# A bidirectional encoder layer on one core: the short convolution's matrices kept, the modulation's tail moved, rows of y loaded one step ahead

## The chip, the cores and the metric

One NeuronCore of a Trainium2 chip runs the whole kernel. The metric is device time in microseconds, the median of several executions. The engines are TensorE (PE, with its weight loads PEld), VectorE (DVE), ScalarE (ACT), GpSimd (POOL) and SyncE (SP), whose queue issues nearly all DMAs here, one after the other.

## The reference, cut to what matters

One layer runs over two sequences, the long one (A, 1024 rows) and the short one (B, 512 rows), with the same weights and width 1024. For each of them:

```
mod = silu(c) @ ada_w + ada_b          # six sections of 1024: sh1 sc1 gt1 sh2 sc2 gt2
u   = rmsnorm(x) * (1 + sc1) + sh1
z   = u @ w_in                         # hyena part, q, k, v, two gates
y_hy = x0 * long_conv(x1 * v, filter)  # FFT convolution over the whole length
y_at = dilated_attention(q, k, v)
h   = x + gt1 * ((g_hy * (y_hy @ w_hy_br) + g_at * (y_at @ w_at_br)) @ w_out)
out = h + gt2 * (relu(u2 @ w_up)**2 @ w_down),   u2 = rmsnorm(h) * (1 + sc2) + sh2
```

## The kernel before, in words

**Products.** Every product is a list of *units*, one unit for 128 output columns. A unit's weights (512 KB) are loaded by SP, split by ACT (L401, a rounded high part) and DVE (L402, the rest), and multiplied in three passes (`mm3`, L768: high by high, high by low, low by high). `stream` walks over the units in the order qkvA and zhyA mixed, gateA, qkvB, zhyB, gateB, mixA, mixB, ffA, ffB. At the start of unit i it splits the weights of unit i+1, then issues unit i's matmuls.

**Side work.** Filters, convolutions, attention, norms, the modulation's rest and loads are generators (`Side`). Between the matmuls of a unit `pump` advances a model clock and lets the first side in the list that is ready issue its next step; `yield c, lat` says what the step costs TensorE and how long the side then isn't ready. `finish` drives a side to its end, moving the model clock on where nothing is ready. A side started with `first=True` stands ahead of the others. This walk sets the program order. ACT executes exactly in program order; for the other engines and for SP a scheduler orders the instructions by that priority and its own estimate of what is ready, and each engine then executes its list strictly in order.

**Buffers.** Most working tiles are one kind, `g`, with 36 buffers of 128x1024 floats; a tile's buffer is given to a later tile when its last reader is done, and that later tile's writer waits for it. The DFT matrices of the convolutions are tiles `cm` with 4 buffers.

**Convolution.** `conv_gen(S, th)` handles a third (256) of the channels; three thirds per sequence, one at a time. `stage1` transposes and does a small DFT; `middle(eg)` loads the intermediate (L921), the filter's spectrum (L971, L972), a forward and a backward matrix (`cmat`, L907 to L910, 256 KB each), multiplies (L984), combines on DVE (L985 to L988), multiplies back (L995), copies on ACT (L388) and writes to DRAM (L1001); then the result is read again (L1008), finished by matmuls L1020 and DVE L1024 and stored as `yhy`. The long sequence has four `eg` per third, the short one two, and every third loads the same matrices again.

**Modulation.** The first two sections are computed at the head. `ada_rest` (L613), started at the first unit of gateA, does the other four: it loads both condition rows, applies silu (ACT L619, DVE L620), then takes 32 steps, each one load of 512 KB (L625) a step ahead and two reductions on DVE (L636, one per sequence). The first unit of mixA's output product waits for its end (`finish(H["ada"])`).

**y.** `load_y(S)` (L1419) brings the convolution's six result tiles back: one DMA (L1425), a pause of 3 us of the model clock, then the split on ACT and DVE. For the long sequence it is started at gateB's unit 12 of 16 and must be through before the first unit of mixA.

Of the kernel before, what the change touches and what calls it, by code (L numbers as in the profile page):

```python
# [337 lines left out]
def _program(ctx, tc, d, outs):  # L338
# [10 lines left out]
    dma = nc.sync.dma_start  # L349
# [14 lines left out]
    def nm(s):  # L364
        cnt[0] += 1
        return f"{phase[0]}__{s}{cnt[0]}"

    def g(shape=(1024,), dt=F32):
        return gp.tile([128, *shape], dt, tag="g", name=nm("g"))
# [7 lines left out]
    def pss2():  # L377
        return pss().rearrange("p (a b) -> p a b", a=2)
# [6 lines left out]
    def copy(out, in_):  # L385
        rr[0] += 1
        if rr[0] % CPM:
            A.copy(out, in_)  # L388
        else:
            V.tensor_copy(out, in_)  # L390
# [4 lines left out]
    def table(name):  # L395
        if held[0] != name:
            A.preload_act_table_set(name)
            held[0] = name

    def split(raw, hi, lo, eng=None):  # L400
        A.copy(hi, raw)  # L401
        (eng or V).tensor_tensor(lo, raw, hi.bitcast(F32), ALU.subtract)  # L402
# [131 lines left out]
    SA, SB = Seq(), Seq()  # L534
# [76 lines left out]
        return mm.ins  # L611

    def ada_rest():  # L613
        csl = [g((1024,)) for _ in range(2)]
        for i in range(2):
            sg = g((1024,))
            dma(csl[i], d["cc"][i:i + 1].broadcast_to([128, 1024]))
            table(SIGMOID)
            A.activation(sg, csl[i], AF.Sigmoid)  # L619
            V.tensor_tensor(csl[i], csl[i], sg, ALU.mult)  # L620
        wt = []

        def load(c):
            t = g((1024,))
            dma(t, d["ada"][c - 16])  # L625
            wt.append(t)

        load(16)
        yield 0.0, 5.0
        for c in range(16, 48):  # L630
            if c < 47:
                load(c + 1)
            junk = g((1024,))
            w = wt.pop(0)
            for i in range(2):
                V.tensor_tensor_reduce(junk, w, csl[i], 1.0, adab[:, c:c + 1], ALU.mult, ALU.add, ada[:, i, c:c + 1])  # L636
            yield 0.0, LADA
        ada_scale(1)

    def ada_scale(n, k0=0, nk=8):  # L640
        gg = (n1g, n2g)[n]
        sc = 8 * (1, 4)[n] + k0
        for i in range(2):
            V.scalar_tensor_tensor(modA[:, n, i, k0:k0 + nk], ada[:, i, sc:sc + nk], 1.0, gg[:, k0:k0 + nk],
                                   ALU.add, ALU.mult)
# [181 lines left out]
    def filt_third(S, th, sall, fwo):  # L827
# [62 lines left out]
        def stage2(eg):  # L890
            sin = stage2_load(S, s1, eg)
            cm = cmat(S.fw, eg)
            yield 0.0, LLD
            so = g((4, 256))
            for ep in range(2):
                ps = pss2()
                for ee in range(2):
                    e = 2 * ep + ee
                    T.matmul(ps[:, ee], cm[:, e], sin[:, e], start=True, stop=True)
                V.tensor_tensor(so[:, 2 * ep:2 * ep + 2], ps, rn.unsqueeze(1).broadcast_to([128, 2, 256]), ALU.mult)  # L900
                yield 0.9, 0.0
            dma(S.spec[th][:, 4 * eg:4 * eg + 4], so)

        yield from par([stage2(eg) for eg in range(nt // 4)], WS2)
        yield 0.0, 3.0

    def cmat(src, eg):  # L907
        cm = wp.tile([128, 4, 128], F32, tag="cm", name=nm("cm"), bufs=4)
        dma(cm, src[eg])
        return cm  # L910

    def stage2_load(S, s1, eg):

        Q, nt = S.Q, S.nt
        nl = 64 // Q
        v = s1.rearrange("j p c -> (j p) c").rearrange("(q r l e) c -> r l q e c", q=Q, r=2, l=nl, e=nt)
        t = g((4, 256))
        for r in range(2):
            for l in range(nl):
                p0 = 64 * r + Q * l  # L920
                dma(t[p0:p0 + Q], v[r, l][:, 4 * eg:4 * eg + 4])  # L921
        return t
# [4 lines left out]
    def conv_gen(S, th):  # L927
# [38 lines left out]
        def middle(eg):  # L966
            sin = stage2_load(S, s1, eg)
            ka, kb = g((4, 256)), g((4, 256))
            es = slice(4 * eg, 4 * eg + 4)
            for hf in range(2):  # L970
                dma(ka[64 * hf:64 * hf + 64], S.spec[th][0:64, es])  # L971
                dma(kb[64 * hf:64 * hf + 64], S.spec[th][64:128, es])  # L972
            if eg == 0:
                V.tensor_copy(ka[64:65, 0], kb[0:1, 0])
                V.memset(kb[0:1, 0], 0.0)
                V.memset(kb[64:65, 0], 0.0)
            cm, cb_ = cmat(S.fw, eg), cmat(S.bw, eg)
            yield 0.0, LLD
            y, vv = g((4, 256)), g((4, 256))
            for ep in range(2):  # L980
                e2 = slice(2 * ep, 2 * ep + 2)
                ps = pss2()
                for ee in range(2):
                    T.matmul(ps[:, ee], cm[:, 2 * ep + ee], sin[:, 2 * ep + ee], start=True, stop=True)  # L984
                V.tensor_tensor(y[:, e2], ps, ka[:, e2], ALU.mult)  # L985
                V.scalar_tensor_tensor(vv[0:64, e2], ps[64:128], -1.0, kb[0:64, e2], ALU.mult, ALU.mult)
                V.tensor_tensor(vv[64:128, e2], ps[0:64], kb[64:128, e2], ALU.mult)
                V.tensor_tensor(y[:, e2], y[:, e2], vv[:, e2], ALU.add)  # L988
                yield 0.9, LY if ep else 0.0
            del sin, ka, kb, vv  # L990
            so = g((4, 256))
            for ep in range(2):
                ps = pss2()
                for ee in range(2):
                    T.matmul(ps[:, ee], cb_[:, 2 * ep + ee], y[:, 2 * ep + ee], start=True, stop=True)  # L995
                copy(so[:, 2 * ep:2 * ep + 2], ps)
                yield 0.9, 0.0
            for r in range(2):
                for l in range(nl):
                    p0 = 64 * r + Q * l  # L1000
                    dma(v2[r, l][:, 4 * eg:4 * eg + 4], so[p0:p0 + Q])  # L1001

        yield from par([middle(eg) for eg in range(nt // 4)], WMID)
        bt = []
        v3 = s2.rearrange("(j q) r c -> (q r) j c", q=4)
        for jg in range(J // 4):
            t = g((4, 256))
# [410 lines left out]

    def load_y(S):  # L1419
        S.yh, S.yl = Feat(S, F32R), Feat(S, F32R)  # L1420
        for k in range(6):
            if k == 5 and S is SA:
                S.gl = {0: load_gate(S, 0)}
            t = g((S.L,))
            dma(t, S.yhy[k])  # L1425
            yield 0.0, 3.0
            split(t, S.yh(k), S.yl(k))

    def load_gate(S, m):
        gs = []  # L1430
        for b in range(2):
            t = g((S.L,))
            dma(t, S.gt[2 * m + b])
            gs.append(t)
        return gs
# [136 lines left out]
    H = {}  # L1572
# [25 lines left out]
    def g0():  # L1598
        H["ada"] = start("ada", ada_rest())
# [28 lines left out]
    def yA():  # L1628
        finish(*(H["convA", th] for th in range(3)), H["combA"])
        H["yA"] = start("mixA", load_y(SA), True)  # L1630
# [11 lines left out]
    def o6():  # L1642
        finish(*(H["convB", th] for th in range(3)), H["combB"])
        H["yB"] = start("mixB", load_y(SB), True)
# [85 lines left out]
def build(arrays):  # L1730
    nc = bacc.Bacc("TRN2", target_bir_lowering=False, num_devices=1)
    d = {n: nc.dram_tensor(n, a.shape, mybir.dt.from_np(a.dtype), kind="ExternalInput").ap()
         for n, a in arrays.items()}
    outs = [nc.dram_tensor(n, s, F32, kind="ExternalOutput").ap()
            for n, s in (("out_a", (8, 128, LA)), ("out_b", (8, 128, LB)))]
    with tile.TileContext(nc) as tc:
        with ExitStack() as ctx:
            ctx.enter_context(tc.manual_schedule(engines={mybir.EngineType.Activation}))
            _program(ctx, tc, d, outs)
    return nc  # L1740
# [10 lines left out]
```

## Time and profile before

| what | value |
|---|---|
| three executions | 2626.16, 2627.82 (median), 2630.31 us |
| profiled execution, its own time | 2630.32 us |
| its span | 2628.5 us, so 1.8 us lie around it |
| mean granted TensorE clock over the span | 0.99 |
| TensorE busy | 2562.4 us (97%) |
| VectorE / ScalarE / GpSimd busy | 1248.1 / 860.8 / 152.0 us |
| moved by DMA | 351.06 MB, mean 134 GB/s |

TensorE is busy almost all the time, so little is left to shares; what can change is read from the few stretches in which it stands still, and from the stretches behind them in which its granted clock is 0.50, that is 1.2 instead of 2.4 GHz. The product stages lie at 647 to 861 us (gateA), 861 to 1010 (qkvB), 1010 to 1144 (zhyB), 1144 to 1264 (gateB), 1281 to 1476 (mixA), 1476 to 1578 (mixB), and from there to the end ffA and ffB.

### The profile page before, as it was taken

The numbers are of one execution on the slowest core, as the hardware profiler recorded it, in microseconds if no ns is written. First come the engines' busy times: TensorE is split into PE (matmuls) and PEld (weight loads), VectorE is DVE, ScalarE is ACT, GpSimd is POOL, SyncE is SP. The second block draws the span as 40 slices with busy tenths as digits, with TensorE's granted clock in tenths as the row PEclk, the third lists the DMA queues.
The fourth block names the chain that finished last, engine by engine and source line by source line (L and its number), as shares of the span: only waits on it lengthen the run. The fifth ranks groups of instructions, "written<-read, shape, count | busy, mean of one in ns | idle before, by whom it ended". The sixth has DMA issues, their size and how long they took to land.

```text
span 2628.5 us, 31915 instructions
## 1 busy us (share of the span) xinstructions
PE 2562.4 (97%) x12872; PEld 2061.4 (78%) x12872; DVE 1248.1 (47%) x1626; ACT 860.8 (33%) x1398; POOL 152.0 (6%) x122
## 2 busy tenths in 40 slices
PE   8999999999899999999899989999999999999999
PEld 4677788787788677787788868888888888888887
DVE  4354443744657644653455563333333332554544
ACT  5544323532422444443332442112211221323232
POOL 0111000000010310000022210000000000000000
PEclk9999999999999999999899999999999999999999
DMA  7455575556565344557563531111111112322223
GB/s 269 143 158 182 185 192 169 151 177 175 190 229 188 110 161 141 157 177 233 190 214 114 189 100 61 48 48 49 48 48 48 49 48 80 129 97 96 98 95 104
DMA packets 138106, 351.06 MB, mean 134 GB/s; under 512 B 19016, under 2 KB 50303, under 8 KB 137830
## 3 DMA queue, kind: packets, MB, share of 16 engines
q1 hardware_dynamic: 137670, 348.22, 41.1%
q8 instruction: 102, 1.67, 0.3%
q0 software_dynamic: 288, 0.79, 0.1%
q14 instruction: 46, 0.38, 0.0%
HBM read 280.67 MB, written 71.16 MB: 134 GB/s over the span
## 4 chain that ended last, share of the span: by engine, by line
PE 50%; DVE 1%; DMA 1%; ACT 0%; issue 0%; SPq 0%; DVEq 0%; ACTq 0%
PE ffA__mm L768 27%; PE ffB__mm L768 13%; PE mixA__mm L768 6%; PE mixB__mm L768 2%; PE convB__s L1020 0%; DMA mixA__g<-zhyA__dr 0%; PE gateB__mm L768 0%; DVE mixB__wl L402 0%; ACT mixB__wh L401 0%; PE convB__s L995 0%; DVE mixA__g L402 0%; PE convB__s L984 0%; DMA convB__g<-convB__dr 0%; DVE normA__g L735 0%; DVE mixB__g L1491 0%
## 5 line engine op out<-in xcount | busy, mean ns | idle before, releaser
L768 PE MATMUL ffA__mm<-ffA__g,ffA__wh 128*128 128x512 f32 x1024 | 274.1, 389 | 0.0
L768 PE MATMUL ffA__mm<-normA__g,ffA__wh 128*128 128x512 f32 x992 | 265.1, 389 | 0.0
L768 PEld LDWEIGHTS ffA__mm<-ffA__g,ffA__wh 128*128 128x128 f32 x1024 | 192.0, 188 | 40.4 <-issue 0.4
L768 PEld LDWEIGHTS ffA__mm<-normA__g,ffA__wh 128*128 128x128 f32 x992 | 186.2, 188 | 38.6
L1529 DVE SCALAR_TENSOR_TENSOR mixA__g<-ffA__mm,adam,mixA__g 128x1024 f32<-128x1024 f32 x64 | 82.1, 1283 | 190.1 <-PE ffA__mm L768 190.1
L768 PE MATMUL ffB__mm<-ffB__g,ffB__wh 128*128 128x512 f32 x512 | 157.8, 389 | 0.0
L768 PE MATMUL ffA__mm<-ffA__g,ffA__wl 128*128 128x512 f32 x512 | 157.7, 389 | 0.0
L768 PE MATMUL ffB__mm<-normB__g,ffB__wh 128*128 128x512 f32 x496 | 152.7, 389 | 0.0
L768 PE MATMUL ffA__mm<-normA__g,ffA__wl 128*128 128x512 f32 x496 | 152.7, 389 | 0.0
L401 ACT CAST ffA__wh<-ffA__wr 128x1024 fp32r<-128x1024 f32 x63 | 66.2, 1051 | 256.7 <-PE ffA__mm L768 213.6
L768 PE MATMUL zhyA__mm<-init__g,zhyA__wh 128*128 128x512 f32 x512 | 145.2, 400 | 0.0
L1511 DVE SCALAR_TENSOR_TENSOR ffA__g<-ffA__mm,ffA__g 128x1024 f32<-128x1024 f32 x32 | 39.2, 1224 | 222.8 <-ACT ffA__g L1510 222.8
L768 PE MATMUL gateA__mm<-init__g,gateA__wh 128*128 128x512 f32 x480 | 133.4, 398 | 7.5 <-ACT gateA__wh L401 7.5
L768 PE MATMUL mixA__mm<-mixA__g,mixA__wh 128*128 128x512 f32 x424 | 115.3, 392 | 3.1 <-DVE mixA__g L1463 1.9
L768 PE MATMUL qkvA__mm<-init__g,qkvA__wh 128*128 128x512 f32 x416 | 116.9, 399 | 0.0
L768 PEld LDWEIGHTS zhyA__mm<-init__g,zhyA__wh 128*128 128x128 f32 x512 | 94.2, 188 | 23.6 <-issue 5.7
L768 PEld LDWEIGHTS ffB__mm<-ffB__g,ffB__wh 128*128 128x128 f32 x512 | 96.0, 188 | 20.3 <-ACT ffB__g L401 0.2
L768 PEld LDWEIGHTS gateA__mm<-init__g,gateA__wh 128*128 128x128 f32 x480 | 90.5, 191 | 27.2 <-ACT gateA__wh L401 7.9
L768 PEld LDWEIGHTS ffA__mm<-ffA__g,ffA__wl 128*128 128x128 f32 x512 | 96.1, 188 | 20.0
L1510 ACT ACTIVATE ffA__g<-ffA__mm 128x1024 f32<-128x1024 f32 x32 | 32.9, 1029 | 237.8 <-PE ffA__mm L768 237.8
L768 PEld LDWEIGHTS ffB__mm<-normB__g,ffB__wh 128*128 128x128 f32 x496 | 93.1, 188 | 19.4
L768 PEld LDWEIGHTS ffA__mm<-normA__g,ffA__wl 128*128 128x128 f32 x496 | 93.1, 188 | 19.3
(499 smaller groups left out, 4926.7 us busy)
## 6 DMA issues: line engine op xcount, KB each, us to landing
ada__g<-ada SPq DMA_DIRECT2D x32, 512.0 KB
ffA__wr<-w_up SPq DMA_DIRECT2D x32, 512.0 KB
ffA__wr<-w_dn SPq DMA_DIRECT2D x32, 512.0 KB
ffB__wr<-w_dn SPq DMA_DIRECT2D x32, 512.0 KB
ffB__wr<-w_up SPq DMA_DIRECT2D x30, 512.0 KB
filtA__dr<-filtA__g SPq DMA_DIRECT2D x24, 512.0 KB
convA__g<-filtA__dr SPq DMA_DIRECT2D x48, 256.0 KB
init__g<-ada SPq DMA_DIRECT2D x16, 512.0 KB
```

The lines of the kernel that those rows point to most:

```text
L401: A.copy(hi, raw)
L768: T.matmul(ps[:, 512 * c:512 * c + 512], ww[:, sl], xx(k)[:, 512 * c:512 * c + 512], start=k == 0 and p == 0, stop=k == kt - 1 and p == 2)
L1510: A.activation(r, ps[:, :L], AF.Relu)
L1511: V.scalar_tensor_tensor(r, ps[:, :L], 0.0, r, ALU.max, ALU.mult)
L1529: V.scalar_tensor_tensor(S.h(m), ps[:, :L], mod(S, 5, m), S.h(m), ALU.mult, ALU.add)
```

## The change

Three edits. `ada_rest` polls, each poll a step of no cost and 1 us of pause, until the three convolutions of the long sequence have issued their last step. `cmats` keeps the short sequence's two pairs of matrices (four tiles, all buffers of `cm`) for all of its thirds. `load_y` issues the DMA of tile k+1 before the split of tile k, with seven pauses in place of six; the first gate load now stands behind the sixth DMA instead of ahead of it.

```diff
     def ada_rest():
+        while not all(H["convA", th].done for th in range(3)):
+            yield 0.0, 1.0
         csl = [g((1024,)) for _ in range(2)]
...
+    kept = {}
+
+    def cmats(S, eg):
+
+        if S is SA:
+            return cmat(S.fw, eg), cmat(S.bw, eg)
+        if eg not in kept:
+            kept[eg] = cmat(S.fw, eg), cmat(S.bw, eg)
+        return kept[eg]
+
...
-            cm, cb_ = cmat(S.fw, eg), cmat(S.bw, eg)
+            cm, cb_ = cmats(S, eg)
...
         S.yh, S.yl = Feat(S, F32R), Feat(S, F32R)
-        for k in range(6):
+        ts = []
+        for k in range(7):
+            if k < 6:
+                t = g((S.L,))
+                dma(t, S.yhy[k])
+                ts.append(t)
             if k == 5 and S is SA:
                 S.gl = {0: load_gate(S, 0)}
-            t = g((S.L,))
-            dma(t, S.yhy[k])
             yield 0.0, 3.0
-            split(t, S.yh(k), S.yl(k))
+            if k:
+                split(ts.pop(0), S.yh(k - 1), S.yl(k - 1))
```

## Rows read from the trace of the kernel before

**Rows 1.** The page of the profile, engines over the span: busy us, share, instructions

```profile
PE 2562.4 (97%) x12872; PEld 2061.4 (78%) x12872; DVE 1248.1 (47%) x1626; ACT 860.8 (33%) x1398; POOL 152.0 (6%) x122
```

**Rows 2.** What the matmul engine waited for, whole span: us, times, longest

```profile
PE convB__s L1020 <- DMA convB__g<-convB__dr: 8.8, 1, 8.8
PE gateA__mm L768 <- ACT gateA__wh L401: 7.5, 1, 7.5
PE gateB__mm L768 <- ACT gateB__wh L401: 3.9, 1, 3.9
```

**Rows 3.** Short stretches: us, busy PE, PEld, DVE, ACT, POOL; granted clock; DMA share, GB/s

```profile
676.87:684.35 7.48, 0.00 (x1) 0.01 (x1) 5.38 (x16) 2.00 (x3) 0.00 (x0) 0.73 0.88 287
684.35:690.52 6.17, 6.01 (x18) 4.16 (x19) 2.73 (x4) 6.16 (x26) 0.00 (x0) 0.50 0.83 332
861.00:905.00 44.00, 38.59 (x206) 28.78 (x205) 29.14 (x62) 21.82 (x39) 12.70 (x10) 0.96 0.36 117
...
1247.72:1253.72 6.00, 5.66 (x13) 3.97 (x13) 5.88 (x8) 3.46 (x4) 0.00 (x0) 0.50 0.40 123
1263.85:1272.62 8.77, 0.00 (x1) 0.04 (x1) 4.61 (x4) 4.21 (x7) 0.00 (x0) 0.70 0.68 205
1272.62:1284.44 11.82, 11.82 (x48) 11.14 (x49) 2.18 (x2) 5.94 (x7) 0.00 (x0) 0.50 0.94 344
```

**Rows 4.** ScalarE in order of time, 630 to 710 us

```profile
656.18 1.06 ACT L619 ACTIVATE ada__g<-ada__g 128x1024 f32<-128x1024 f32 x1 [5.30 <-DMA ada__g<-cc]
659.44 1.06 ACT L619 ACTIVATE ada__g<-ada__g 128x1024 f32<-128x1024 f32 x1 [2.19 <-DMA ada__g<-cc]
...
682.34 1.01 ACT L388 COPY gateA__g<-gateA__mm 128x1024 f32<-128x1024 f32 x1 [10.01 <-DVE adam L636]
683.25 1.05 ACT L401 CAST gateA__wh<-gateA__wr 128x1024 fp32r<-128x1024 f32 x1
```

**Rows 5.** VectorE in order of time, 640 to 700 us

```profile
682.17 0.08 DVE L636 DVE_READ_ACCUMULATOR2_ANT adam<- 128x1 f32 x1
```

**Rows 6.** SyncE's DMA issues in order of time, 1140 to 1320 us

```profile
1236.57 0.39 SPq L1425 DMA_DIRECT2D mixA__g<-zhyA__dr  x1
...
1257.48 0.33 SPq L909 DMA_DIRECT2D convB__cm<-c_bw_b  x1
1257.91 0.38 SPq L1425 DMA_DIRECT2D mixA__g<-zhyA__dr  x1
```

**Rows 7.** What ScalarE waited for, 1190 to 1300 us

```profile
ACT mixA__g L401 <- DMA mixA__g<-zhyA__dr: 35.3, 5, 13.3
```

**Rows 8.** VectorE in order of time, 1190 to 1320 us

```profile
1246.27 1.23 DVE L402 TENSOR_TENSOR mixA__g<-mixA__g,mixA__g 128x1024 fp32r<-128x1024 f32 x1 [13.07 <-DMA mixA__g<-zhyA__dr]
1247.41 0.68 DVE L985 TENSOR_TENSOR convB__g<-convB__s,convB__g 128x512 f32<-128x512 f32 x1
```

**Rows 9.** What SyncE's queue waited for, 1220 to 1300 us

```profile
SPq L909 <- PE convB__s L995: 9.9, 1, 9.9
SPq L909 <- PE convB__s L984: 3.6, 2, 3.2
```

**Rows 10.** Loads of the matrices' tile, 1100 to 1400 us

```profile
L909 SPq DMA_DIRECT2D convB__cm<-c_fw_b x4: 332/391/411, 1158.6 to 1241.1; - x4
L909 SPq DMA_DIRECT2D convB__cm<-c_bw_b x4: 328/358/771, 1178.3 to 1257.5; - x4
```

**Rows 11.** The reductions' line L636 on VectorE, 705 to 870 us

```profile
L636 DVE CUSTOM_DVE_ANT_0 ada__g<-ada__g,ada__g,prm x58: 1268/1284/2412, 705.5 to 862.7; 128x1024 f32<-128x1024 f32 x58
```

**Rows 12.** Stages around the change, the same columns

```profile
704.00:861.00 157.00, 156.48 (x738) 127.52 (x738) 111.29 (x179) 49.84 (x94) 14.99 (x11) 1.00 0.62 213
861.00:925.00 64.00, 57.59 (x341) 42.20 (x339) 41.24 (x77) 33.44 (x61) 18.83 (x16) 0.97 0.31 100
...
1400.00:1476.00 76.00, 76.00 (x339) 62.94 (x338) 34.51 (x29) 19.48 (x24) 19.52 (x10) 1.00 0.44 149
```

**Rows 13.** VectorE in order of time, 774 to 793 us

```profile
775.80 2.32 DVE L636 CUSTOM_DVE_ANT_0 ada__g<-ada__g,ada__g,prm 128x1024 f32<-128x1024 f32 x1
```

## The prediction

> **What bounds the kernel now.** The page first: TensorE is busy 97% of the span [rows 1], so its matmuls set the time and a change of side work can only win or lose the stretches in which it stands still. The view of waits names them: of what TensorE waits for after the head, three waits are large, 8.8, 7.5 and 3.9 us, each occurring once [rows 2]. The view of busy time by stretch shows the price of each beyond the wait itself [rows 3]: after a stretch without matmuls the granted clock falls to 0.50, the 1.2 GHz level, and the matmuls behind it take twice their time (6.17 us, 6.00 us and 11.82 us at that level). Half of such a stretch is lost. Then the views in order of time tell what each wait hangs on.
>
> *The wait at 676.87 us.* TensorE waits for the split of the next gate weights, ScalarE's L401 at 683.25. That stands behind the copy L388, which had waited 10.01 us for a buffer [rows 4] whose last reader was the modulation's reduction L636, done at 682.25 [rows 5]. Here the modulation does harm.
>
> *The wait that ends at 1247.72 us and the one from 1263.85 on.* ScalarE waits 35.3 us, five times, for loads of y [rows 7]: `load_y` issues a load and then its split, and ScalarE, in strict order, holds the next weights' split behind it. VectorE is held likewise, 13.07 us, with the convolution's L985 right behind [rows 8], so the short convolution's second third comes late too. SyncE makes it worse: it waits 9.9 and 3.2 us for a free buffer of the DFT matrices [rows 9], and the fourth row of y is issued only after that, at 1257.91 instead of some 10 us earlier [rows 6]. The late convolution then has its last read land too late for L1020: the 8.8 us.
>
> **The change part by part.** The sum goes against the profiled execution, 2630.3 us, which lies 2.5 us above the median; the parts' gains are taken off that and the 2.5 us at the end.
>
> *Modulation, where it leaves.* From 649 to about 705 us it no longer runs, and the buffer that the copy waited for isn't held. I take the whole wait, 7.48 us, and half of the 6.17 us at the lower clock, 3.1: **-10.6**. Bounds: -10.6, and 0 if another holder of a `g` buffer is as late; the copy waited for nothing else in that row, so I stay at the first end.
>
> *Modulation, where it starts.* Its two activations L619 waited 5.30 and 2.19 us for the condition rows [rows 4], at a place where TensorE had other work. Moved, they fall at about 706 us, where ScalarE goes over to attention's exponentials. A wait of 7.5 us on ScalarE there holds the exponentials, a gate's copy and the next weights. It costs 0 if the loads are issued early enough and at most the 7.5 us and some at the lower clock, say 8; I take **+2.5**, near the lower end, since the earlier such wait cost TensorE nothing.
>
> *Modulation, where it ends.* After 705 us the old kernel made 58 of its 64 reductions up to 862.7 [rows 11], 29 steps in 157 us, 5.4 us each, and TensorE was busy 156.48 of 157.00 us beside them [rows 12]. So in gateA a step costs nothing. Starting at about 715 us, 26 or 27 steps fit ahead of 861; some 6 steps, 12 reductions, are pushed into the stretch 861 to 905, which had two. VectorE was busy 29.14 of 44.00 us there [rows 3]; less two and plus twelve reductions of 1.284 us it is 29.14 + 12.8 = 42 us, practically all of it, and 861 to 925 is the stretch in which TensorE already loses 6.4 us to chains of short steps [rows 12]. A reduction in front of such a step delays it by about half its length on average, 12 x 0.64 = 7.7 us, of which the matmuls of qkvB cover some: I take **+6**. Bounds: 0, if all fall into gaps; and above, the third rival's price. The 6 loads of 512 KB and the five buffers held longer are counted at nothing: the DMA share in 861 to 905 is 0.36 [rows 3]. If SyncE's queue stands behind a store, a reduction waits for its load with everything behind it; that belongs to the third rival.
>
> *Matrices kept.* Between 1100 and 1400 us eight loads of 256 KB go [rows 10] and with them SyncE's 9.9 and 3.2 us of waiting [rows 9]. Alone that moves nothing on TensorE except through y: the fourth row could be issued about 10 us earlier. No term of its own; the rest of the convolution's queue stays.
>
> *y one ahead, first gap.* Between a load and its split now lie two pauses, 6 us of the model clock, in place of one. At the pace of two splits in a unit the first no longer stands in gateB's unit 12 but in unit 13, behind the weights' split that TensorE lacked: the 3.9 us [rows 2] and half of 6.00 us [rows 3] go. **-6.9**; bounds -6.9 and, if the load still lands late, 0.
>
> *y one ahead, second gap.* With VectorE free, L985 need not wait [rows 8] and the convolution's copies, store and read come 6 to 10 us sooner, against a wait of 8.77 us. In full it is 8.77 and half of 11.82: -14.7. Against that stands the seventh pause, which pushes the last splits nearer to mixA. I leave 2.5 us of wait and 1.2 of clock: **-11**; bounds -14.7 and 0.
>
> *y of the short sequence.* The same code runs within mixA's output units, where TensorE is busy 76.00 of 76.00 us [rows 12]: 0, covered by those matmuls. One pause more of 3 us has four units of room.
>
> Sum: -10.6 + 2.5 + 6 - 6.9 - 11 = -20.0, so 2610.3 for the profiled execution and, 2.5 below it, 2607.8 for a median: **2608 us**.
>
> **Rivals.**
>
> *First: the second gap stays.* The scheduler places L1020 ahead of mixA's first matmuls, and if its read is again late, or the last row of y is (seven pauses, not six), the 14.7 us remain. For it: the order of L1020 is the scheduler's, not the program's, and a step is added to a loader that has only four units. Against: both things that held the read, VectorE and the queue, are gone. Without the -11 the sum is -9.0, which gives 2618.8.
>
> *Second: the tail cancels.* The chains of 861 to 925 lose about what the wait at 676.87 gave, 9 to 14 us, the start costs its full 8, and y gives only its first gap. -10.6 + 8 + 9 to 14 - 6.9 is -0.5 to +4.5, or 2627 to 2632. For it: VectorE's 42 of 44 us. Against: all three have to come together.
>
> *Third: VectorE becomes the bound behind gateA (slower).* Place: 861 to 925 us. Of the reductions the one at 775.80 took 2.32 us and the longest 2.41 instead of 1.28 [rows 11, 13], in the stretch in which GpSimd adds up squares; in 861 to 905 GpSimd is busy 12.70 us with attention's sums [rows 3]. If every one of the twelve meets an addition, VectorE has 12 x 2.41 = 28.9 in place of two times 1.28, that is 29.14 + 26.4 = 55.5 us in 44, and the chains, each behind the other, see all 26.4 that are added. With the clock at 0.50 over some 20 us of it, ten more: +36. 2630.3 - 10.6 - 17.9 + 2.5 + 36 = 2640.3, or 2638 as a median. It decides once the added delay passes 26 us, twelve reductions at 2.2 us each, all on the path. Against it: the median of the 58 is 1.284 us [rows 11], and beside gateA's matmuls even the long ones cost nothing. The Trainium skill (SBUF — State Buffer, Who interferes with whom) has this as a rule: a DVE instruction with two SBUF inputs contends with a GpSimd instruction that reads SBUF. The trace agrees with it in the 2.32 us; by the rule alone every overlap would cost, and how many overlap no run here shows yet.
>
> *Fourth: the edits only move the program's order.* The scheduler might issue the same loads and reductions where it did. The activations on ScalarE follow the program's order, so this can't hold for the first and third edit; counted within the second rival.
>
> **How the numbers follow.** 0.2%, or 5.3 us, is about what a measurement of this kernel can tell from no change. The forecast has 0.53, the first rival 0.17 (both faster); the second 0.15, nearly all within 5.3 us; the third 0.15. So faster 0.70, same 0.14, slower 0.16, a little being moved to the slower side for the second rival's end. The range begins at 2595, where both gaps of y and the first wait go in full and the moved work costs nothing (-10.6 - 6.9 - 14.7 = -32.2 on 2627.8), and reaches to 2634, which takes in the first two rivals and leaves out the third. The likeliest case alone has 2595 to 2617.
>
> **What would show it.** Right: no wait for `gateA__wh` near 677 us and granted clock 1.00 there; L636 from about 715 to about 900 us; no load of `convB__cm` after the first third; ScalarE's 35.3 us for y under 10; the 8.8 us of L1020 under 3. Wrong in the tail: waits of qkvB's or combine's matmuls on VectorE above 10 us in total in 861 to 925, with L636 above 2 us. Wrong in y: a wait of L1020 or of mixA's first unit that is still above 5 us. The forecast fails as a whole if the time is above 2622.

## The result, and the profile after

| what | before | after |
|---|---|---|
| median | 2627.32 us (2626.16 to 2630.31) | 2609.49 us (2607.94 to 2612.07) |
| ratio of the times | | 0.9934, interval 0.9922 to 0.9947 |
| profiled execution, its span | 2630.32, 2628.5 us | 2608.41, 2606.6 us |

Four executions of each were timed. The changed kernel is faster by 17.8 us. TensorE issues as many matmuls as before [rows 1]; what it saves is time in which it stood still and time at the low clock. Line numbers behind the edits move: L636 becomes L638, L768 becomes L770, L1020 becomes L1032, L1354 becomes L1366. The page, engines over the span:

```profile
PE 2551.0 (98%) x12872; PEld 2051.2 (79%) x12872; DVE 1249.3 (48%) x1626; ACT 861.3 (33%) x1398; POOL 152.0 (6%) x122
```

Where the time went is read by stage: from the first matmul of a product to the first of the next one. Busy time by stretch, before, for gateA, qkvB, zhyB and gateB (the columns of [rows 3]; the stretch of gateB runs up to mixA's first matmul):

```profile
647.40:860.90 213.50, 205.34 (x1033) 168.12 (x1032) 137.23 (x229) 71.69 (x150) 14.90 (x11) 0.98 0.62 211
860.90:1010.50 149.60, 143.19 (x876) 106.94 (x875) 82.24 (x149) 74.25 (x146) 26.80 (x26) 0.99 0.42 133
1010.50:1144.30 133.80, 133.80 (x807) 106.27 (x806) 79.03 (x133) 65.76 (x160) 7.57 (x5) 1.00 0.44 138
1144.30:1281.00 136.70, 121.22 (x545) 99.67 (x544) 56.15 (x70) 41.63 (x58) 0.00 (x0) 0.93 0.71 225
```

The same four stages after:

```profile
647.28:849.03 201.75, 201.75 (x1034) 166.20 (x1033) 125.73 (x209) 72.09 (x150) 13.27 (x9) 1.00 0.60 210
849.03:1006.08 157.05, 145.64 (x875) 107.10 (x874) 93.46 (x169) 74.12 (x146) 28.33 (x27) 0.97 0.44 143
1006.08:1139.91 133.83, 133.83 (x806) 106.27 (x805) 79.09 (x133) 65.80 (x160) 7.57 (x5) 1.00 0.43 138
1139.91:1261.01 121.10, 114.16 (x545) 94.08 (x544) 55.39 (x69) 41.40 (x57) 0.00 (x0) 1.00 0.72 225
```

gateA is 11.75 us shorter, qkvB 7.45 us longer, zhyB the same, gateB 15.6 us shorter. Everything behind is 1.9 us shorter in all. The change gives in two places, as the waits promised, and takes in one.

What TensorE waited for over the whole span, after (us, times, longest), the rows that bear on the change:

```profile
PE combineA__s L1364 <- DVE attA__g L1366: 5.4, 2, 3.5
...
PE convB__s L1032 <- DMA convB__g<-convB__dr: 2.5, 1, 2.5
PE qkvB__s L664 <- DVE attA__g L1366: 1.9, 1, 1.9
```

Of the three large waits [rows 2], the 7.5 us for `gateA__wh` and the 3.9 us for `gateB__wh` are gone, and the 8.8 us of the convolution's last read is 2.5 us. New are 7.3 us (5.4 and 1.9) on VectorE's L1366, the products of `combine`, the step that weights and adds the parts of the long sequence's attention; there 2.0 us stood before. Short stretches after:

```profile
676.87:684.35 7.48, 7.48 (x64) 7.12 (x62) 1.57 (x3) 1.17 (x2) 0.00 (x0) 1.00 0.34 137
861.00:905.00 44.00, 33.49 (x170) 22.63 (x171) 34.30 (x70) 19.38 (x37) 12.66 (x10) 0.88 0.23 80
884.00:894.20 10.20, 6.74 (x15) 3.63 (x16) 8.98 (x13) 5.37 (x8) 6.57 (x6) 0.50 0.38 132
1253.71:1261.01 7.30, 4.77 (x42) 4.42 (x41) 1.45 (x2) 2.32 (x3) 0.00 (x0) 1.00 1.05 346
```

The 7.48 us of 676.87 that had no matmul [rows 3] now hold 64 of them at clock 1.00. In 861 to 905 VectorE is busy 34.30 us instead of 29.14 and the clock is 0.88 instead of 0.96, because 10.2 us of it ran at 0.50. The last stretch holds the 2.5 us wait, which ends at 1256.62, and the matmuls behind it; it comes back below.

The reductions, the loads of the matrices' tile and ScalarE's wait for y (one row or two of one view each):

```profile
L638 DVE CUSTOM_DVE_ANT_0 ada__g<-ada__g,ada__g,prm x64: 1269/1284/2411, 701.7 to 880.6; 128x1024 f32<-128x1024 f32 x64
```

```profile
L921 SPq DMA_DIRECT2D convB__cm<-c_fw_b x2: 328/340/352, 1018.1 to 1078.1; - x2
L921 SPq DMA_DIRECT2D convB__cm<-c_bw_b x2: 443/872/1302, 1026.6 to 1084.2; - x2
```

```profile
ACT mixA__g L401 <- DMA mixA__g<-zhyA__dr: 12.3, 3, 7.6
```

The reductions run from 701.7 to 880.6 instead of up to 862.7 [rows 11]. No matrix is loaded after 1084.2, where eight loads went before [rows 10]. ScalarE waits 12.3 us for y instead of 35.3 [rows 7].

### The profile page after: what moved, and what is told of

Read it like the earlier page. It is cut to its first block, busy times and chain, and to the rows that moved or that the text cites. A ratio compares the mean times of both kernels' runs of the same rounds, so it can differ in the third digit from the quotient of the medians.

```text
span 2606.6 us, 31910 instructions
## 1 busy us (share of the span) xinstructions
PE 2551.0 (98%) x12872; PEld 2051.2 (79%) x12872; DVE 1249.3 (48%) x1626; ACT 861.3 (33%) x1398; POOL 152.0 (6%) x122
## 4 chain that ended last, share of the span: by engine, by line
PE 69%; DVE 2%; DMA 1%; ACT 1%; issue 1%; POOL 0%; SPq 0%; DVEq 0%; ACTq 0%; POOLq 0%
PE ffA__mm L770 27%; PE ffB__mm L770 13%; PE gateA__mm L770 7%; PE mixA__mm L770 6%; PE zhyB__mm L770 4%; PE qkvB__mm L770 3%; PE mixB__mm L770 2%; PE gateB__mm L770 2%; PE filtB__s L901 0%; DVE mixB__wl L402 0%; PE convB__s L1007 0%; DMA convB__g<-convB__dr 0%; PE attB__s L1290 0%; DMA mixA__g<-zhyA__dr 0%; PE convB__s L996 0%
## 5 line engine op out<-in xcount | busy, mean ns | idle before, releaser
L770 PE MATMUL ffA__mm<-ffA__g,ffA__wh 128*128 128x512 f32 x1024 | 274.1, 389 | 0.0
L770 PE MATMUL ffA__mm<-normA__g,ffA__wh 128*128 128x512 f32 x992 | 265.1, 389 | 0.0
L770 PEld LDWEIGHTS ffA__mm<-ffA__g,ffA__wh 128*128 128x128 f32 x1024 | 192.0, 188 | 40.5 <-issue 0.4
L770 PEld LDWEIGHTS ffA__mm<-normA__g,ffA__wh 128*128 128x128 f32 x992 | 186.2, 188 | 38.7
L770 PE MATMUL ffB__mm<-ffB__g,ffB__wh 128*128 128x512 f32 x512 | 157.8, 389 | 0.0
L770 PE MATMUL ffA__mm<-ffA__g,ffA__wl 128*128 128x512 f32 x512 | 157.7, 389 | 0.0
L770 PE MATMUL ffB__mm<-normB__g,ffB__wh 128*128 128x512 f32 x496 | 152.7, 389 | 0.0
L770 PE MATMUL ffA__mm<-normA__g,ffA__wl 128*128 128x512 f32 x496 | 152.7, 389 | 0.0
L770 PE MATMUL zhyA__mm<-init__g,zhyA__wh 128*128 128x512 f32 x512 | 145.2, 400 | 0.0
L770 PE MATMUL gateA__mm<-init__g,gateA__wh 128*128 128x512 f32 x480 | 132.0, 394 | 0.0
L770 PE MATMUL mixA__mm<-mixA__g,mixA__wh 128*128 128x512 f32 x424 | 115.3, 392 | 3.1 <-DVE mixA__g L1479 1.9
L770 PE MATMUL qkvA__mm<-init__g,qkvA__wh 128*128 128x512 f32 x416 | 117.0, 399 | 0.0
L770 PEld LDWEIGHTS zhyA__mm<-init__g,zhyA__wh 128*128 128x128 f32 x512 | 94.2, 188 | 23.6 <-issue 5.7
L770 PEld LDWEIGHTS ffB__mm<-ffB__g,ffB__wh 128*128 128x128 f32 x512 | 96.0, 188 | 20.2 <-ACT ffB__g L401 0.2
L770 PEld LDWEIGHTS ffA__mm<-ffA__g,ffA__wl 128*128 128x128 f32 x512 | 96.1, 188 | 20.0
L770 PEld LDWEIGHTS ffA__mm<-normA__g,ffA__wl 128*128 128x128 f32 x496 | 93.1, 188 | 19.3
L770 PEld LDWEIGHTS ffB__mm<-normB__g,ffB__wh 128*128 128x128 f32 x496 | 93.1, 188 | 19.3
L770 PEld LDWEIGHTS gateA__mm<-init__g,gateA__wh 128*128 128x128 f32 x480 | 89.5, 188 | 20.2 <-issue 1.3
```

The lines of the kernel that those rows point to most:

```text
L770: T.matmul(ps[:, 512 * c:512 * c + 512], ww[:, sl], xx(k)[:, 512 * c:512 * c + 512], start=k == 0 and p == 0, stop=k == kt - 1 and p == 2)
```

## The experiments

Ten kernels, in three groups, each group beside runs of the kernel before on the same chip. All but the changed kernel itself differ from the kernel before or after by a few lines. A stage is measured as above, in the one profiled execution, which need not be a typical one: that of "second and third" is the slowest of its four (2618.0 us against 2613.1 to 2613.6), and that of "pause in combine" the fastest of its five (2606.6 us, the others up to 2611.1).

| kernel | median us | ratio | interval | gateA | qkvB | zhyB | gateB |
|---|---|---|---|---|---|---|---|
| before | 2626.57, 2628.0, 2625.81 | 1 | | 213.5 | 149.5 | 133.8 | 136.8 |
| first edit alone | 2624.36 | 0.9994 | 0.9985 to 1.0003 | 201.7 | 157.0 | 133.9 | 137.1 |
| third edit alone | 2615.81 | 0.9958 | 0.9943 to 0.9972 | 212.0 | 149.4 | 133.8 | 124.2 |
| second edit alone | 2618.34 | 0.9968 | 0.9956 to 0.9980 | 211.6 | 150.4 | 133.8 | 128.3 |
| second and third | 2613.58 | 0.9949 | 0.9932 to 0.9965 | 212.8 | 149.3 | 133.8 | 126.1 |
| all three, again | 2611.28 | 0.9940 | 0.9928 to 0.9952 | 201.7 | 157.1 | 133.8 | 124.4 |
| pause in combine | 2610.03 | 0.9929 | 0.9917 to 0.9942 | 201.7 | 153.2 | 133.8 | 124.6 |
| faster steps | 2608.35 | 0.9923 | 0.9910 to 0.9937 | 206.9 | 149.3 | 133.8 | 124.7 |
| faster steps, y earlier | 2607.27 | 0.9923 | 0.9910 to 0.9937 | 206.4 | 149.3 | 133.9 | 121.4 |
| pause into zhyB | 2609.07 | 0.9934 | 0.9921 to 0.9946 | 201.7 | 149.9 | 138.8 | 125.3 |
| pause into zhyB, y earlier | 2608.77 | 0.9934 | 0.9920 to 0.9947 | 201.7 | 149.7 | 138.9 | 119.0 |

The first four ran beside the median 2626.57, the next four beside 2628.0, the last two beside 2625.81.

**The modulation alone.** Only the two lines of `ada_rest`:

```diff
     def ada_rest():
+        while not all(H["convA", th].done for th in range(3)):
+            yield 0.0, 1.0
```

> Only the first edit: the modulation's rest behind the long sequence's convolutions; matrices and y as before. Theory (three stretches that add up): the wait at 677 us and its low clock go, some -11.5 us, and the stretch behind gateA loses some +7.5 us, so -4 us against before, ratio 0.9985; the two waits of 3.9 and 8.8 us at gateB's end stay. Rival (the modulation's place moves nothing by itself, the whole gain is y's): no wait goes, 0 to +8 us. Rival (the tail's loss comes only from the three edits together): -11 us, ratio 0.996.

The ratio can't be told from 1: some 2 us by the medians, where the stages in the table make it 4. TensorE's waits from 640 to 1300 us:

```profile
PE convB__s L1022 <- DMA convB__g<-convB__dr: 8.4, 1, 8.4
PE combineA__s L1354 <- DVE attA__g L1356: 5.1, 2, 3.5
PE gateB__mm L770 <- ACT gateB__wh L401: 4.3, 1, 4.3
```

The wait at 677 us is gone and gateA is 11.8 us shorter; 7.5 us of it are given back in qkvB, where `combine` (L1354 here) waits 5.1 us and the clock is 0.50 for 13.7 us from 881.4 on. Both gaps at the end of gateB stay. So the modulation's gain and the tail's loss are this edit's own, and the rest of the 17.8 us is y's and the matrices'.

**y alone.** Only `load_y` from the diff.

> Only the third edit: rows of y loaded one ahead; modulation and matrices as before. Theory (ScalarE's waits for y carry both gaps, SyncE's waits for matrices are a smaller part): the wait of 3.9 us goes, the one of 8.8 us falls to 3 to 6 us, -10 to -15 us against before, ratio 0.9945 to 0.996. Rival (the matrices' waits on SyncE hold the convolution's reads, and y too): the second gap stays at 8 us or more, -7 us, ratio 0.9975. Rival (y alone does it all): -17 us, ratio 0.9935.

10.8 us faster. The same view:

```profile
PE convB__s L1020 <- DMA convB__g<-convB__dr: 2.6, 1, 2.6
```

The first gap at gateB's end is gone, the second is 2.6 us, and the wait of 7.5 us at 677 us stands as before. `combine` is at its old 2.0 us.

**The matrices alone.** Only `cmats` and its call.

> Only the second edit: the short sequence's four matrix tiles kept; modulation and y as before. Theory (the first load of y still holds ScalarE 13 us, only the fourth row of y is issued up to 10 us sooner): the 3.9 us stay, the 8.8 us shrink by some, -2 to -6 us against before, ratio 0.998 to 0.9992. Rival (it moves nothing without the third edit): 0. Rival (SyncE's waits are the cause): -12 us or more.

8.2 us faster, more than I had expected of it. The same view, and then ScalarE in order of time:

```profile
PE gateB__mm L768 <- ACT gateB__wh L401: 4.6, 1, 4.6
...
PE convB__s L1030 <- DMA convB__g<-convB__dr: 1.9, 1, 1.9
```

```profile
1253.83 0.59 ACT L388 COPY convB__g<-convB__s 128x512 f32<-128x512 f32 x1 [1.63 <-PE convB__s L1005]
1255.16 0.59 ACT L388 COPY convB__g<-convB__s 128x512 f32<-128x512 f32 x1 [0.75 <-PE convB__s L1005]
1256.08 1.05 ACT L401 CAST mixA__g<-mixA__g 128x1024 fp32r<-128x1024 f32 x1 [0.34 <-DMA mixA__g<-zhyA__dr]
```

The first gap stays (4.6 us), but the second is 1.9 us, as small as with y's own edit. ScalarE's row in the kernel before tells why:

```profile
1262.84 1.05 ACT L401 CAST mixA__g<-mixA__g 128x1024 fp32r<-128x1024 f32 x1 [9.43 <-DMA mixA__g<-zhyA__dr]
1263.79 1.06 ACT L388 COPY convB__g<-convB__s 128x512 f32<-128x512 f32 x2
```

There ScalarE stood 9.43 us for a row of y, the one that SyncE had issued only after its 9.9 us wait for a matrix buffer [rows 6, 9], and the convolution's two copies stood behind it in ScalarE's order and came at 1263.79. Without matrix loads SyncE isn't held, and the copies come at 1253.83 and 1255.16, ahead of the split. So the second gap hung on one chain, buffer wait, late load, late split, late copy, and it can be cut at two places.

VectorE was held in this kernel as long as before. In order of time:

```profile
1244.25 1.23 DVE L402 TENSOR_TENSOR mixA__g<-mixA__g,mixA__g 128x1024 fp32r<-128x1024 f32 x1 [13.59 <-ACT mixA__g L401]
1245.39 0.68 DVE L995 TENSOR_TENSOR convB__g<-convB__s,convB__g 128x512 f32<-128x512 f32 x1
```

It stood 13.59 us (13.07 before [rows 8]) with the convolution's first product right behind (L995 here, L985 before), and the second gap closed all the same. So VectorE's hold alone does not make that gap.

**y and the matrices.** Both, without the modulation.

> Second and third edit, the modulation where it was. Theory: -17 us against before, ratio 0.9935, with the 7.5 us at 677 us still there and no loss behind gateA; so it stands some 4 us above the kernel with all three edits. Rival (the modulation's move is of no use on the whole, its tail takes all it gives): the same time as with all three edits, 2609 us or below.

13.0 us, where the two alone gave 10.8 and 8.2: they don't add, since both take the second gap. Its ratio is 0.9949, that of all three edits 0.9934 and 0.9940, so the modulation is worth some 2 to 4 us, less than the intervals tell apart; the stages say the same, -11.8 + 7.5.

**All three, again.** The changed kernel beside the variants that follow.

> The changed kernel once more, so that the next three stand beside it on the same chip. Expected: ratio to before 0.993 to 0.9945, a loss of some 7.5 us behind gateA against the same stretch of before.

**A pause in the tail.** While `combine` runs, the modulation makes no step:

```diff
             yield 0.0, LADA
+            while "combA" in H and not H["combA"].done:
+                yield 0.0, 1.0
```

> All three edits, and the modulation's steps stand still from the start of the long sequence's combination to its end; the buffers it holds (condition rows, the loaded weights) stay held meanwhile. Theory (the loss behind gateA comes from reductions standing in VectorE's order in front of the combination's products): the waits on attA L1366 (3.5, 1.9 and 1.9 us) fall below 2 us each, -4 to -8 us against all three edits. Rival (the loss comes from the g buffers held longer): no gain, within 2 us, or a loss. Rival (the reductions now collide with the short filter's steps instead): -2 to +4 us.

TensorE's waits from 640 to 1300 us, and the reductions' line:

```profile
PE qkvB__s L666 <- ACT qkvB__g L1142: 2.8, 1, 2.8
...
PE combineA__s L1366 <- DVE attA__g L1368: 2.0, 2, 1.4
```

```profile
L638 DVE CUSTOM_DVE_ANT_0 ada__g<-ada__g,ada__g,prm x64: 1267/1284/2411, 700.6 to 922.2; 128x1024 f32<-128x1024 f32 x64
```

`combine` is back at 2.0 us, and the clock over qkvB is 1.00. But qkvB is only 3.9 of the 7.5 us shorter: the reductions now end at 922.2, still within it, and 3.7 us stay there. The wait of 2.8 us on ScalarE was 1.3 us before, but it is 2.4 and 2.9 us with y or the matrices alone, whose qkvB takes 149.4 and 150.4 us, so it is not the reductions' doing. New are 1.3 us of waiting for the norm of qkvB's rows behind it (L692), whose steps on VectorE stand behind two of the moved reductions (893.0 and 894.3). With the reductions out of `combine` its extra wait is gone, so it was they that it waited behind. VectorE in order of time in the changed kernel has the picture (start, us, operation):

```profile
869.16 1.28 DVE L638 CUSTOM_DVE_ANT_0 ada__g<-ada__g,ada__g,prm 128x1024 f32<-128x1024 f32 x1
...
870.75 1.27 DVE L638 CUSTOM_DVE_ANT_0 ada__g<-ada__g,ada__g,prm 128x1024 f32<-128x1024 f32 x1
...
872.03 1.88 DVE L1366 TENSOR_TENSOR attA__g<-combineA__s,attA__g 128x512 f32<-128x512 f32 x3
...
879.15 1.28 DVE L638 CUSTOM_DVE_ANT_0 ada__g<-ada__g,ada__g,prm 128x1024 f32<-128x1024 f32 x1
...
880.65 1.28 DVE L638 CUSTOM_DVE_ANT_0 ada__g<-ada__g,ada__g,prm 128x1024 f32<-128x1024 f32 x1
...
882.27 0.68 DVE L1366 TENSOR_TENSOR attA__g<-combineA__s,attA__g 128x512 f32<-128x512 f32 x1
```

Two reductions, 1.28 and 1.27 us, stand just ahead of the first products of `combine`, and two more ahead of the product at 882.27, the one that TensorE's longest wait (3.5 us, ending at 883.01) was for.

**Faster steps.** The modulation's steps 3.5 instead of 4 us of the model clock apart:

```diff
-LADA = 4.0
+LADA = 3.5
```

> All three edits, with the model's pause between two steps of the modulation 3.5 instead of 4 us, so that the 32 steps end ahead of gateA's end. Theory (beside gateA's matmuls a reduction costs nothing, the loss lies only behind gateA): the last reduction ends before 850 us, the stretch behind gateA loses what it lost before the change or less, -6 to -8 us against all three edits, about 2602 us. Rival (denser reductions hold up gateA's own splits): gateA's stage grows by 3 us or more and takes it back.

The last reduction is at 848.7, before qkvB begins. TensorE's waits, ScalarE's split in the norm of the short sequence, and gateA by stretch:

```profile
PE normB__s L690 <- ACT normB__g L401: 2.1, 1, 2.1
PE combineA__s L1364 <- DVE attA__g L1366: 2.0, 2, 1.4
```

```profile
794.36 0.40 ACT L401 CAST normB__g<-normB__g 64x256 fp32r<-64x256 f32 x1 [6.26 <-DVE normB__g L656]
```

```profile
646.80:853.70 206.90, 203.56 (x1033) 167.34 (x1032) 141.80 (x233) 72.19 (x150) 15.62 (x11) 0.99 0.65 220
```

qkvB is as before the change, 149.3 us, and `combine` waits 2.0 us. But gateA is 5.2 us longer, with waits in that norm and the clock at 0.99. ScalarE waits 6.26 us there for the norm's step L656 on VectorE, instead of 3.69 us in the changed kernel: between ScalarE's own last step of the norm and L656 VectorE runs three reductions and a split of weights, where there were two reductions.

**The tail out of the way.** The pause held on until the short sequence's first convolution starts; what the modulation has in hand then keeps its buffers some 200 us longer:

```diff
             yield 0.0, LADA
+            while "combA" in H and ("convB", 0) not in H:
+                yield 0.0, 1.0
```

> All three edits, and the modulation's steps stand still from the end of gateA until the short sequence's first convolution starts (some 200 us, the buffers held all the while); the rest of its reductions then run beside zhyB and gateB. Theory (only a reduction ahead of a short step's VectorE work costs, held buffers don't): the qkvB stage takes what it took before the change, about 148.5 in place of 156.1 us, the later stages stay as they are, -7 us against all three edits, ratio to before about 0.9915. Rival (held buffers cost): qkvB and zhyB lose 3 us or more by waits on SyncE or ScalarE for buffers. Rival (a reduction costs some 0.6 us of TensorE's time wherever it is put): -3 us at most.

```profile
PE zhyB__mm L772 <- DVE zhyB__g L1058: 2.8, 2, 2.7
...
PE combineA__s L1366 <- DVE attA__g L1368: 1.9, 2, 1.4
```

qkvB is 149.9 us, so the buffers held across it cost nothing. But zhyB is 5.0 us longer, with a wait of 2.7 us on VectorE, which was busy 14.93 of the 15 us up to that wait's end, four of the reductions among its work.

The modulation's last steps thus cost TensorE 3.7 us behind `combine`, 5.0 in zhyB, 5.2 when pressed into gateA, and 7.5 beside `combine`. By the intervals none of the three variants is told from the change, whose two are 0.9922 to 0.9947 and 0.9928 to 0.9952. Beside the changed kernel on the same chip the faster steps do come out ahead: their four executions took 2604.0 to 2609.1 us, its five 2611.1 to 2613.4, with medians 2.9 us apart, against 6 to 8 us expected.

**y earlier.** In two of the variants y is started earlier than at gateB's unit 12 (`YAU = 10` with the faster steps, `YAU = 11` with the long pause):

> As the kernel with the denser modulation, and y of the long sequence started at gateB's unit 10 instead of 12. Theory (the convolution's last read is still 2.5 us late because y's splits stand in front of its copies and sums): the waits of L1032 (2.5 us) and L1007 (1.5 us) go, -2 to -5 us more. Rival (the wait is the DMA's own way from the store to the read): no further gain. Rival (twelve more buffers taken two units earlier): a loss of 3 us or more, with waits on SyncE for buffers.

> As the last one, with y of the long sequence started at gateB's unit 11 instead of 12. Theory (the convolution's last read and the splits of y compete for ScalarE and VectorE in the same few units, so a shift trades one wait for another): the wait of 2.5 us ahead of mixA goes, others of 1 to 4 us come within gateB, the same time within 2 us. Rival (one unit is just the slack that is missing): -3 to -8 us, counting the low clock behind the wait.

No gain. With the faster steps the wait for the convolution's last read (2.8 us there) is no longer among the large ones, but the convolution's middle waits instead (the two waits were 2.1 and 1.8 us before this shift):

```profile
PE convB__s L996 <- DMA convB__g<-convB__dr: 4.0, 2, 3.0
PE convB__s L1007 <- DVE convB__g L1000: 3.8, 1, 3.8
```

With the long pause the wait for the last read stays, 3.0 us. gateB is 3 to 6 us shorter and mixA 3 to 4 us longer (196.6 and 197.3 us against 193.7 and 193.5).

## Why the prediction was right, and where its steps were off

The forecast was 2608 us, the median is 2609.5; for the profiled execution it was 2610.3, and that took 2608.4. The sum of -20.0 met -21.9, or -17.8 by the medians, with terms that partly missed:

- **Modulation, where it leaves: -10.6.** gateA gave -11.75: it takes 201.7 us with this edit alone and with all three. The four kernels without the edit have 211.6 to 213.5, so the gain is 9.9 to 11.8. Right: wait and clock, both.
- **Modulation, where it starts: +2.5.** It cost nothing. ScalarE in order of time, after:

```profile
697.03 1.28 ACT L397 ACT_TABLE_LOAD   x1
698.33 2.01 ACT L621 ACTIVATE ada__g<-ada__g 128x1024 f32<-128x1024 f32 x2
...
701.31 1.28 ACT L397 ACT_TABLE_LOAD   x1
```

The two activations waited for nothing: their loads had landed. They now stand between attention's exponentials with a table load of 1.28 us on either side (16 such loads in the whole span, as before), and TensorE waited 0.6 us in all from 640 to 720.

- **Modulation, where it ends: +6.** qkvB lost 7.45. The place and the mechanism were right, reductions in front of short steps of attention. So was the count, twelve behind gateA, but by two errors that cancel: they begin at 701.7 instead of about 715, and gateA ends at 849.03, where I had counted up to its old end, 861. Only six fall in 861 to 905, and VectorE is busy 34.3 us there and not the 42 that I had put. I had averaged half a reduction over all of them; it was a few waits of up to 3.5 us and then the clock, PE busy 145.64 against 143.19 us for the same products, 2.45 us of the 7.45.
- **In gateA a step costs nothing.** True at 5.4 us a step, and at some 5.7 us in the changed kernel, whose gateA has TensorE busy 201.75 of 201.75 us. At the quicker pace, some 4.7 us a step, gateA lost 5.2 us, so the sentence doesn't hold for more steps in the same time.
- **Matrices kept: no term of their own.** This step failed on its own terms: alone they gave 8.2 us. The prediction had named the link ("except through y: the fourth row"), and left out what stood behind that row, the convolution's copies in ScalarE's order. The sum did not suffer, since y takes the same gap.
- **y, first gap -6.9 and second -11.** Together -17.9; gateB gave -15.6 and mixA -1.6, -17.2. That match is in part luck: in the second run of the changed kernel the same two stages gave -12.4 and -0.3, and second and third edit together gave 13.0 by the medians, so this term was probably some 5 us too large, and it was the start's +2.5, which cost nothing, that made up for a part. The 2.5 us of wait that I had left in the second gap are measured as 2.5. The way was wrong: I gave the whole second gap to y by way of VectorE, but with the matrices alone VectorE is held as before, 13.59 us, and the gap is 1.9 us. What held it was ScalarE's copies behind a late split, and either edit nearly closes it.
- **y of the short sequence: 0.** mixA lost nothing. Right.
- **ScalarE's wait for y under 10 us.** 12.3 us, in three. A sign that was missed; no product of gateB waits for ScalarE's split behind it.

The rivals. The first, that the second gap stays, did not come. The second, that the tail cancels, came true for the first edit taken alone (-11.8 + 7.5, a ratio not told from 1), but not beside y's gain. The third, that VectorE becomes the bound, did not come: none of the twelve late reductions met an addition of GpSimd, and none took over 1.29 us. Its condition was real: with the pause in `combine` three late reductions did meet GpSimd's additions for the short filter (from 901.6 to 910.2) and took 1.71, 1.70 and 2.17 us. The four long ones lie in gateA, where they had been seen [rows 13]; two of them, on VectorE, and what GpSimd does meanwhile, in order of time after:

```profile
774.92 2.31 DVE L638 CUSTOM_DVE_ANT_0 ada__g<-ada__g,ada__g,prm 128x1024 f32<-128x1024 f32 x1
...
777.27 2.19 DVE L638 CUSTOM_DVE_ANT_0 ada__g<-ada__g,ada__g,prm 128x1024 f32<-128x1024 f32 x1
```

```profile
774.41 7.57 POOL L702 TENSOR_TENSOR normB__g<-normB__g,normB__g 128x512 f32<-128x512 f32 x4 [4.26 <-ACT normB__g L701]
```

The Trainium skill (SBUF — State Buffer, Who interferes with whom) has it that a DVE instruction with two SBUF inputs contends with a GpSimd instruction that reads SBUF. The trace agrees as to these: 2.31 and 2.19 us beside the additions, about 1.28 where no addition runs, and no loss on TensorE from it.

## What to carry to other kernels

Follow a wait through every strictly ordered queue that it passes, and price each link: where one chain can be cut in two places, the two gains don't add, and either edit looks idle only beside the other. Side work that is moved is paid for where it lands, so count its instructions in the new place against the short chains there, not against the long products; here its last ten to twelve reductions cost 4 to 8 us at each of three places behind gateA, and pressing them into gateA cost 5. Judge parts by stage lengths: an edit that gave 11.8 us and took 7.5 looked like nothing as a total.

## What was not expected of the hardware

The same short wait did not always cost clock. Ahead of L1032 TensorE waited 2.5 us in the changed kernel, and the matmuls behind it ran at 1.00 (1253.71 to 1261.01, above). In the second run of the same program it waited 2.62 us there, until 1255.97, and this stretch followed:

```profile
1256.20:1266.40 10.20, 10.20 (x45) 9.79 (x45) 2.09 (x2) 5.64 (x6) 0.00 (x0) 0.50 1.03 399
```

For 10.2 us the clock is 0.50 with TensorE busy throughout, half of which, 5.1 us, is lost; gateB took 124.4 instead of 121.1 us and mixA 194.3 instead of 193.1. These two gaps differ by less than 0.1 us, and these 4.5 us are a part of what the program's executions differ by. Two gaps ahead of qkvB's matmul L666 say more: with the pause in `combine` TensorE waited 2.83 us there, and with the long pause 2.34 us. The stretches behind them, in this order:

```profile
890.20:899.66 9.46, 7.66 (x60) 5.01 (x61) 7.67 (x12) 5.90 (x12) 0.00 (x0) 1.00 0.33 111
```

```profile
892.59:895.59 3.00, 3.00 (x37) 0.97 (x37) 1.82 (x3) 2.94 (x8) 0.00 (x0) 0.50 0.08 30
```

The longer gap was followed by the full clock and the shorter one by the low one, so the length of a gap alone does not decide which comes.
